# S5 parameters in large stores, later state loads, one weight spill and a carried-over stage in a hybrid streaming encoder step

## Chip, cores and metric

The kernel runs on 1 core of one Trainium2 chip. The metric is the device time of one execution in microseconds (us); less is better. The five engines are TensorE (PE), VectorE (DVE), ScalarE (ACT), GpSimd (POOL) and SyncE (SP). SP and POOL issue the transfers here.

## What is computed

One layer of a two-branch encoder on 2048 prompt frames and 8 x 16 sample frames of width 1024, in float32. Cut to what matters:

```python
h = rmsnorm(x, ln_g)
u_a, z_a, u_b, z_b, g_a, g_b = split(h @ w_in)     # 512, 512, 1024, 1024, 1024, 1024 columns
# branch A: S5 with 32 groups of 16 channels, 64 complex states each
y_a = gelu(s5_scan(u_a, state_s5))                 # B, C and lambda of each group, D u
y_a = y_a * sigmoid(y_a @ w_glu + b_glu)
p_a = (y_a * silu(z_a)) @ w_pa
# branch B: causal convolution of width 4, RG-LRU
xc = conv(u_b, state_conv)
y_b = rglru(xc, state_lru)                         # a = exp(-8 r softplus(-lam)), r and i by block-diagonal gates
p_b = (y_b * silu(z_b)) @ w_pb
m = sigmoid(g_a) * p_a + sigmoid(g_b) * p_b
y = rmsnorm(x + m @ w_out)
```

The last states of both recurrences and of the convolution are outputs too.

## The kernel before

**Tiles.** The 2176 frames are five tiles: four of 512 frames and one of 128, the sample (TILES, NT = 5). Each float32 operand is held as two float16 parts, high and low, and each product is three passes (L159 to L161: high x high, high x low, low x high), so a 128x512 product over 1024 rows is 24 matmuls. Five PSUM banks with the tag mm take the products, three with the tag a the small ones.

**Stages.** (1) The frames are normed and transposed, and u_a is computed (uE, four tiles of 8704 bytes per partition, m = 0 to 3). During the fourth tile SP stores each uE[m] to uD (L594) while POOL and DVE finish the S5 parameters in the job `params`, which ends with nine stores by SP to the DRAM tile parD (L513 to L523). parD holds 16 sets of 453 numbers per partition, so each store is cut into 128 x 16 pieces of 4 to 512 bytes. (2) The pools of stage 1 close, and the pools pgb (pages) and gp open on their memory; gp has 21 slots with the tag g, which `gt` takes, on the side where uE lay. The first lines after this load the states of the LRU and the convolution and clear and fill the small tile dn (L630 to L642). (3) Two loops over the five tiles compute gate B's first four column blocks (`direct`), with W0, then with W1; beside them run the jobs `t_forms`, which form the sums of a Strassen-Winograd product, and the splitting of W1. In the second loop, after tile 2, `lru_states` transposes the states on PE. (4) Branch B: 16 pairs of column blocks, 8 of branch B in turn with 8 of the gates (`run_pair`, seven products for each half of the tiles, positions 1 to 7 and 9 to 15, the sample at 8). (5) Projection B (y_b @ w_pb): the loop over n and m, 24 matmuls each. (6) The GLU and projection A (`ga_tile`: 4 products with w_glu, then 8 with w_pa), and the output (`out_tile`).

**What sets the order.** The program is issued in the order in which it is written; each engine and each queue takes its instructions in that order. Beside the products runs a planner. Jobs are generators in the lists tasks and low; `pump(budget)` takes one step of each job that is due, tasks first, until the budget is used up. A step that yields Later(k) rests k ticks, Step(c) costs c and rests one tick. A tick comes after each product: 2.4 less what the product's own eviction costs in branch B, 2.2 in projection B (`beside`, twice in each (n, m), once at n = 4). Tiles of a pool are freed by their last use, so a new tile in a slot waits for what used the slot before, a store's landing too.

**The jobs.** `b_work` is the elementwise part and the scan of one block of branch B; its last stage y_lo stores y to ybD (L976). `w_spill` loads 44 blocks of w_pb, w_glu, w_pa and w_out (L1151), splits each into high and low (scopy, stt) and stores it (L1159); it is put into low twice: before `load_pair(0)`, and again with `s5_prep` after tile 2 of the second loop. `s5_prep` (two of them, the second from the end of branch B on) reads a parameter set (L1195), rests 3 ticks, and makes the matrices wb and wc, the kernel kf and its shifted form dd of two groups. `s5_run(q)`, 16 jobs that are started 4 ticks apart in projection B, at most three at a time, reads them (sp, u and the phases ph, L1391 to L1395), rests 5 ticks, and runs the scan:

```python
while q not in prepared or running > 2:
    yield Later(1)
running += 1
...
yield Later(5)
...
    running -= g
```

**The end of branch B.** In the last pair, `hook_z` loads the pages of w_pb at positions 8 to 11. At 13 it runs the planner until tasks is empty, loads y_b of tile 0 (`y_load(0)`) and the S5 state (`s5_open`, h0n). After the pair come `s5_init` (two transposes of h0n on PE), `y_load(NT - 1)` and projection B. `out_states` (three transposes on PE, copies `so` on DVE) stands at n = 0, m = 3. Behind the loop `beside` runs until no job is left.

**The GLU operand.** `glu_prep(n)` loads ya, the scan's output of tile n in four parts (L1615), and splits it into yh (8 copies on ACT, 8 subtractions on DVE). For tile 0 it stands ahead of everything; for tile n + 1 it and ga_tile(n + 1) are one chain, of which two steps are taken after each product group of out_tile(n).

Of the kernel before, what the change touches and what calls it, by code (L numbers as in the profile page):

```python
# [43 lines left out]
O_PR, O_PI, O_B, O_BS, O_C, O_CS, O_ER, O_EI, O_M = 0, 34, 68, 100, 132, 164, 196, 324, 452  # L44
NPAR = 453
# [3 lines left out]
def build(tc, I, O):  # L49
# [30 lines left out]
    with ExitStack() as es:  # L80
# [3 lines left out]
        wp = es.enter_context(tc.tile_pool(name="wp", bufs=1))  # L84
# [22 lines left out]
        l16 = cp.tile([P, 2, 16], F32, name="l16")  # L107


        uD = dr.tile([512 * 8, 544], F16, name="uD")  # L110
        parD = dr.tile([16, P, NPAR], F32, name="parD")
# [101 lines left out]
        with ExitStack() as p1x:  # L213
# [25 lines left out]
            m16c = p1.tile([P, 16], F32, name="m16c")  # L239
# [58 lines left out]
            def params():  # L298
# [171 lines left out]
                pv = parD.rearrange("q p x -> p q x")  # L470

# [158 lines left out]
        rows2 = gt([64, P], F32, name="rows2")  # L630
        SP.dma_start(out=rows2, in_=I["state_lru"][0].rearrange("s (b c) -> (s b) c", c=P))
        rows3 = [gt([96, P], F32, name=f"rows3{i}") for i in range(2)]
        cst = I["state_conv"][0].rearrange("s k (b c) -> (s k b) c", c=P)
        for i in range(2):
            SP.dma_start(out=rows3[i], in_=cst[96 * i:96 * i + 96])

        dn = gt([16, 64], name="dn")
        V.memset(dn, 0.0)
        s5d = I["s5_d"][0].rearrange("(q g) h -> q g h", g=2)
        SP.dma_start(out=dn[:, 0:16], in_=s5d[:, 0])  # L640
        SP.dma_start(out=dn[:, 48:64], in_=s5d[:, 1])
        SP.dma_start(out=e16, in_=I["c_e16"])  # L642
# [260 lines left out]

        def b_work(b, ns):
# [69 lines left out]
            def y_lo(n):  # L974
                tt(y[n][:, 1], h.pop(n), y[n][:, 0], SUB)
                G.dma_start(out=ybD[n, b] if n < NT - 1 else ybS[b], in_=y.pop(n))  # L976

# [152 lines left out]
        def w_spill():  # L1130
# [15 lines left out]
            for i, (src, dst, nk) in enumerate(blocks):  # L1146
# [3 lines left out]
                raw = gt([P, nk, 512 // nk], name="wr")  # L1150
                SP.dma_start(out=raw, in_=src)  # L1151
                yield Later(2)
                while busy(NO_SPILL):
                    yield Later(1)
                q = gt([P, nk, 2, 512 // nk], F16, name="wq")
# [3 lines left out]
                G.dma_start(out=dst, in_=q)  # L1159
                yield Step(0.7)  # L1160
            done["spill"] = len(blocks)
# [13 lines left out]
        def s5_prep(second):  # L1175
# [12 lines left out]
            while todo:  # L1188
# [118 lines left out]
        low.append([0, w_spill()])  # L1307
# [3 lines left out]
        for n in range(NT):  # L1311
            for i in range(2):
# [210 lines left out]

        def wpb_load():
            wpb.append(page_load(page_b("t0", (2, KB, 2, P), "wpb"), wpbD[len(wpb)]))

        def y_load(n):
            for h in range(2):
                if n < NT - 1:
# [280 lines left out]
```

## Time and profile before

| | us |
|---|---|
| median of 3 runs | 1629.98 (1626.01 to 1632.69) |
| the profiled execution's own time | 1622.52 |
| its span, first to last instruction | 1620.7 |
| TensorE busy | 1457.7 (90%) |
| VectorE busy | 1063.9 (66%) |
| ScalarE busy | 839.9 (52%) |
| GpSimd busy | 301.7 (19%) |

The profile is of one execution. Its page gives busy times, the span in 40 slices, and the costliest groups; the list of waits tells for whom an engine stood idle; the timeline gives instructions in order of time, with the idle time before them in brackets; stage windows give busy times of a stretch. PEclk is the clock granted to TensorE, 1.00 being 2.4 GHz and 0.50 being 1.2 GHz. A wait for several semaphores is put down to the one that came last.

### The profile page before, as it was taken

What the parts mean: (1) busy time and instruction counts of PE and PEld (TensorE: products, weight loads), DVE (VectorE), ACT (ScalarE), POOL (GpSimd) and SP (SyncE); (2) the same over time, 40 slices, a digit from 0 to 9 for tenths busy, and PEclk for the clock granted to TensorE, in tenths of its full rate; (3) what the DMA queues carried; (4) which work ended last, traced back from release to release, by engine and by line L of the source; (5) the groups of instructions that cost most, each with busy time, mean ns of one, the idle gap of its engine ahead of it and who ended that gap; (6) DMA issues with size and microseconds to landing.
All of it is one profiled execution on the core that took longest, in us unless ns stands there. A gap on an engine that the chain in (4) does not pass through costs nothing.

```text
span 1620.7 us, 23021 instructions
## 1 busy us (share of the span) xinstructions
PE 1457.7 (90%) x8168; PEld 727.1 (45%) x8168; DVE 1063.9 (66%) x2181; ACT 839.9 (52%) x1570; POOL 301.7 (19%) x601
## 2 busy tenths in 40 slices
PE   6992699999989999999999895799999799999997
PEld 4440244444444444444444442355556444343444
DVE  6540585876867686786868685456765775656554
ACT  7540233675857676775858474143434452424232
POOL 0770011021111202020111102244444200000000
PEclk9996799999999999999999997899999799999999
DMA  7229522334342514243333408888978833333432
GB/s 198 88 86 99 126 75 95 103 111 129 109 142 86 165 53 163 88 146 92 114 123 115 141 22 306 319 289 303 308 266 308 314 130 137 122 138 122 138 105 79
DMA packets 194412, 245.31 MB, mean 151 GB/s; under 512 B 42522, under 2 KB 139434, under 8 KB 192376
## 3 DMA queue, kind: packets, MB, share of 16 engines
q1 hardware_dynamic: 166840, 162.51, 34.1%
q0 software_dynamic: 27456, 81.32, 13.7%
q8 instruction: 64, 1.05, 0.3%
q14 instruction: 52, 0.43, 0.1%
HBM read 145.40 MB, written 98.38 MB: 150 GB/s over the span
## 4 chain that ended last, share of the span: by engine, by line
PE 46%; DVE 16%; issue 10%; DMA 6%; ACT 5%; POOL 1%; SPq 1%; POOLq 0%; ACTq 0%; DVEq 0%
PE ps_mm L160 11%; PE ps_mm L161 11%; PE ps_mm L159 11%; PE ps_mm L1729 3%; PE ps_mm L1727 3%; PE ps_mm L1728 3%; DVE xc L66 2%; DVE wf L66 2%; DMA par<-parD 1%; DMA ya<-yDp 1%; DVE q L887 1%; DMA mbD<-gb 1%; DVE yh L54 1%; ACT yh L75 1%; DMA h0n<-state_s 1%
## 5 line engine op out<-in xcount | busy, mean ns | idle before, releaser
L161 PE MATMUL ps_mm<-h,wf 128*128 128x512 f16 x448 | 170.7, 381 | 42.3 <-DVE wf L66 42.3
L159 PE MATMUL ps_mm<-T,wf 128*128 128x512 f16 x512 | 194.5, 380 | 2.2 <-DVE gs L54 1.9
L161 PE MATMUL ps_mm<-T,wf 128*128 128x512 f16 x512 | 194.5, 380 | 1.0 <-DVE wf L66 1.0
L160 PE MATMUL ps_mm<-T,wf 128*128 128x512 f16 x512 | 194.5, 380 | 0.0
L161 PEld LDWEIGHTS <-wf 128*128 128x128 f16 x1232 | 121.3, 98 | 158.3 <-DVE wf L66 44.3
L159 PEld LDWEIGHTS <-wf 128*128 128x128 f16 x1232 | 121.4, 99 | 116.9 <-issue 5.4
L160 PEld LDWEIGHTS <-wf 128*128 128x128 f16 x1232 | 121.3, 98 | 114.8 <-issue 6.6
L159 PE MATMUL ps_mm<-h,wf 128*128 128x512 f16 x448 | 170.9, 381 | 2.0 <-ACT wf L75 2.0
L160 PE MATMUL ps_mm<-h,wf 128*128 128x512 f16 x448 | 170.8, 381 | 0.0
L75 ACT ACT_TABLE_LOAD x64 | 82.1, 1283 | 51.0 <-PE ps_mm L161 49.4
L1729 PE MATMUL ps_mm<-wo,M 128*128 128x512 f16 (+2 forms) x280 | 104.0, 373 | 0.1
L1727 PE MATMUL ps_mm<-wo,M 128*128 128x512 f16 (+2 forms) x280 | 104.1, 373 | 0.0
L1728 PE MATMUL ps_mm<-wo,M 128*128 128x512 f16 (+2 forms) x280 | 104.1, 373 | 0.0
L159 PE MATMUL ps_mm<-Y,wpb 128*128 128x512 f16 x256 | 100.1, 391 | 0.0
L160 PE MATMUL ps_mm<-Y,wpb 128*128 128x512 f16 x256 | 99.6, 389 | 0.0
L161 PE MATMUL ps_mm<-Y,wpb 128*128 128x512 f16 x256 | 99.4, 388 | 0.0
L75 ACT ACTIVATE wq<-wr 128x512 f16<-128x512 f32 x88 | 53.2, 619 | 42.4 <-DMA wr<-w_out 25.8
L66 DVE SCALAR_TENSOR_TENSOR xc<-ub,PC,xc 128x512 f32<-128x512 f32 x96 | 71.9, 749 | 2.3
L66 DVE SCALAR_TENSOR_TENSOR xo<-ps_mm,xo 128x512 f32<-128x512 f32 (+2 forms) x35 | 24.9, 711 | 65.9 <-PE ps_mm L1729 65.9
L66 DVE SCALAR_TENSOR_TENSOR wq<-wr,wq 128x512 f16<-128x512 f32 x88 | 59.1, 685 | 11.4 <-ACT wq L75 11.0
L160 PE MATMUL ps_mm<-yA,wt 128*128 128x512 f16 (+1 forms) x160 | 54.9, 351 | 9.8 <-DVE yA L66 9.8
L66 DVE SCALAR_TENSOR_TENSOR wf<-wraw,wf 128x512 f16<-128x512 f32 (+1 forms) x82 | 55.7, 696 | 10.8 <-ACT wf L75 10.8
(316 smaller groups left out, 3294.9 us busy)
## 6 DMA issues: line engine op xcount, KB each, us to landing
wraw<-w_in SPq DMA_DIRECT2D x38, 512.0 KB, 3.9
sp<-sD SPq DMA_DIRECT2D x16, 768.0 KB, 6.4
xt<-x_prompt SPq DMA_DIRECT2D x16, 512.0 KB, 4.2
gbD<-gs POOLq DMA_DIRECT2D x32, 256.0 KB, 2.4
wr<-w_pb SPq DMA_DIRECT2D x32, 256.0 KB, 3.4
wpbD<-wq POOLq DMA_DIRECT2D x32, 256.0 KB, 3.1
ybD<-y POOLq DMA_DIRECT2D x32, 256.0 KB, 3.3
gaD<-gs POOLq DMA_DIRECT2D x32, 256.0 KB, 2.7
```

The costliest lines, as they stand in the source:

```text
L54: V.tensor_tensor(out=out, in0=a, in1=b, op=op)
L66: V.scalar_tensor_tensor(out=out, in0=a, scalar=s, in1=b, op0=op0, op1=op1)
L75: S.activation(out=out, in_=a, func=f, **kw)
L159: PE.matmul(p, lhsT=a[:, 0], rhs=b[:, 0], start=first, stop=False, skip_group_check=more)
L160: PE.matmul(p, lhsT=a[:, 0], rhs=b[:, 1], start=False, stop=False, skip_group_check=more)
L161: PE.matmul(p, lhsT=a[:, 1], rhs=b[:, 0], start=False, stop=last, skip_group_check=more)
L887: V.tensor_tensor_scan(out=q, data0=a, data1=q, initial=0.0 if n == 0 else prev[:, w - 1:w], op0=MUL, op1=ADD)
L1727: PE.matmul(p, lhsT=lh[0], rhs=w_[:, 0, c], start=(k == 0), stop=False)
L1728: PE.matmul(p, lhsT=lh[0], rhs=w_[:, 1, c], start=False, stop=False)
L1729: PE.matmul(p, lhsT=lh[1], rhs=w_[:, 0, c], start=False, stop=(k == KB - 1))
```

## The change

parD becomes three DRAM tiles with the partition first, written by five stores and read in parts; m16c stays in SBUF (pool cp). The state loads move into `load_states`, which is called at n = 1 of the second loop. One `w_spill` is left; outside branch B it uses tiles of pool wp and loads one block ahead. At the end of branch B the jobs are not run out any more: `y_load` waits (in the program's order) only for the blocks that it reads, `s5_open` moves to position 9, `y_load(NT - 1)` into projection B, `out_states` to n = 1. A parameter set rests 6 ticks outside branch B, a scan's pages 7. `glu_prep` runs a tile further ahead, its subtractions one turn later.

```diff
-        wp = es.enter_context(tc.tile_pool(name="wp", bufs=1))
+        wp = es.enter_context(tc.tile_pool(name="wp", bufs=1, reuse_waits="tile"))
...
-        parD = dr.tile([16, P, NPAR], F32, name="parD")
+        pwD = dr.tile([P, 2, 16, 34], F32, name="pwD")
+        bcD = dr.tile([P, 4, 16, 32], F32, name="bcD")
+        etD = dr.tile([P, 2, 16, P], F32, name="etD")
...
-                SP.dma_start(out=pv[:, :, O_PR:O_PR + 34], in_=pw[:, 0].rearrange("p (q g) e -> p q (g e)", g=2))
-                SP.dma_start(out=pv[:, :, O_PI:O_PI + 34], in_=pw[:, 1].rearrange("p (q g) e -> p q (g e)", g=2))
-                for o, src in ((O_B, bst), (O_BS, bsw)):
-                    SP.dma_start(out=pv[:, :, o:o + 32], in_=src.rearrange("p (q g) h -> p q (g h)", g=2))
-                for o, src in ((O_C, cc[:, 0]), (O_CS, cc[:, 1])):
-                    SP.dma_start(out=pv[:, :, o:o + 32], in_=src.rearrange("p (q x) -> p q x", x=32))
+                SP.dma_start(out=pwD, in_=pw.rearrange("p r (q g) e -> p r q (g e)", g=2))
+                for o, src in enumerate((bst, bsw)):
+                    SP.dma_start(out=bcD[:, o], in_=src.rearrange("p (q g) h -> p q (g h)", g=2))
+                SP.dma_start(out=bcD[:, 2:4], in_=cc.rearrange("p i (q x) -> p i q x", x=32))
                 level(64, 63, tt)
                 yield
-                SP.dma_start(out=pv[:, :, O_ER:O_ER + P], in_=et[:, 0])
-                SP.dma_start(out=pv[:, :, O_EI:O_EI + P], in_=et[:, 1])
-                SP.dma_start(out=pv[:, :, O_M], in_=m16c)
+                SP.dma_start(out=etD, in_=et)
...
+        def load_states():
+            nonlocal rows2, rows3, dn
...
+            dn = gt([16, 64], name="dn")
+            V.memset(dn, 0.0)
...
+                if branch_b:
+                    r = gt([P, nk, 512 // nk], name="wr")
+                else:
+                    r = raw_tile()[:, 0:4].rearrange("p a b -> p (a b)").rearrange("p (k c) -> p k c", k=nk)
...
+                raw = nxt
+                if raw is None:
+                    raw = load(i)
+                    yield Later(2 if branch_b else 6)
+                nxt = None if branch_b or i + 1 == len(blocks) else load(i + 1)
...
+                    q = wp.tile([P, nk, 2, 512 // nk], F16, tag="wt", name="wq", bufs=1)
...
-                par = gt([P, O_ER], name="par")
-                SP.dma_start(out=par, in_=parD[q, :, 0:O_ER])
-                yield Later(3)
+                par = gt([P, NPAR], name="par")
+                SP.dma_start(out=par[:, 0:68].rearrange("p (r e) -> p r e", r=2), in_=pwD[:, :, q])
+                SP.dma_start(out=par[:, 68:196].rearrange("p (i x) -> p i x", i=4), in_=bcD[:, :, q])
+                yield Later(3 if branch_b else 6)
...
-        low.append([0, w_spill()])
         raw = load_pair(0)
...
+            if n == 1:
+                load_states()
...
-            SP.dma_start(out=ph, in_=parD[q, :, O_ER:NPAR])
-            yield Later(5)
+            SP.dma_start(out=ph.rearrange("p (r c) -> p r c", r=2), in_=etD[:, :, q])
+            yield Later(7)
...
         def y_load(n):
+            while (7, n) not in stored:
+                beside()
...
+            if pos == 9:
+                s5_open()
             if pos == 13:
-                while tasks:
-                    clock += 1
-                    pump(1e9)
                 y_load(0)
-                s5_open()
...
-        y_load(NT - 1)
...
-        PAGES = {(0, 2): [lambda: y_load(1)], (0, 6): [lambda: y_load(2)], (1, 2): [lambda: y_load(3)],
+        PAGES = {(0, 1): [lambda: y_load(NT - 1)], (0, 2): [lambda: y_load(1)], (0, 6): [lambda: y_load(2)], (1, 2): [lambda: y_load(3)],
...
-                if n == 0 and m == 3:
+                if n == 1 and m == 3:
                     out_states()
...
-                for j in range(2):
-                    tt(tv[1][:, j], yv[:, j], tv[0][:, j], SUB)
+
+                def low(tv=tv, yv=yv):
+                    for j in range(2):
+                        tt(tv[1][:, j], yv[:, j], tv[0][:, j], SUB)
+                defer(1, low)
...
+        flush()
+        ahead = glu_prep(1)
         for i, _ in enumerate(ga_tile(0)):
...
+            if i > 7:
+                next(ahead, None)
         for n in range(NT):
             flush()
-            nxt = chain(glu_prep(n + 1), ga_tile(n + 1)) if n + 1 < NT else iter(())
-            for _ in out_tile(n):
+            nxt = ga_tile(n + 1) if n + 1 < NT else iter(())
+            for i, _ in enumerate(out_tile(n)):
                 for _ in range(2):
                     pump(0)
                     next(nxt, None)
+                if i == 3 and n + 2 < NT:
+                    ahead = glu_prep(n + 2)
+                if i > 3:
+                    next(ahead, None)
```

## Rows read from the trace of the kernel before

**Rows 1.** The page: busy time, share of the span and instructions of each engine.
```profile
PE 1457.7 (90%) x8168; PEld 727.1 (45%) x8168; DVE 1063.9 (66%) x2181; ACT 839.9 (52%) x1570; POOL 301.7 (19%) x601
```

**Rows 2.** Stage window: length, busy PE, PEld, DVE, ACT, POOL, granted clock, DMA share, GB/s.
```profile
160.00:200.00 40.00, 24.90 (x107) 10.98 (x108) 20.61 (x33) 9.23 (x14) 2.25 (x4) 0.76 0.58 135
```

**Rows 3.** List of waits, 118 to 205 us: us in total, times, longest.
```profile
PE ps_mm L161 <- DVE wf L66: 42.3, 1, 42.3
```

**Rows 4.** Timeline, 118 to 200 us: start, us, engine, line, operation, [idle before <- releaser].
```profile
121.11 3.81 SPq L516 DMA_DIRECT2D parD<-bst  x1
...
162.00 5.88 SPq L594 DMA_DIRECT2D uD<-uE  x2
...
173.38 0.11 DVE L638 MEMSET dn<- 16x64 f32 x1 [41.74 <-DMA uD<-uE]
...
175.10 0.61 PE L161 MATMUL ps_mm<-h,wf 128*128 128x512 f16 x1 [42.34 <-DVE wf L66]
...
178.92 0.41 PE L161 MATMUL ps_mm<-h,wf 128*128 128x512 f16 x1
```

**Rows 5.** List of waits, PE alone, 200 to 960 us: the largest kind.
```profile
PE ps_a L160 <- DVE xs L54: 19.7, 9, 3.9
```

**Rows 6.** List of waits, PE alone, 960 to 1290 us: the four largest kinds.
```profile
PE ps_a L170 <- DVE wb L54: 11.7, 3, 9.0
PE ps_a L1251 <- DVE wc L54: 9.2, 3, 5.5
PE ps_a L170 <- DVE so L1480: 7.9, 1, 7.9
PE ps_a L170 <- DMA h0n<-state_s: 5.6, 1, 5.6
```

**Rows 7.** Timeline, 990 to 1022 us: PE at the carry into projection B.
```profile
998.59 0.38 PE L161 MATMUL ps_mm<-T,wf 128*128 128x512 f16 x1
...
1015.14 0.63 PE L159 MATMUL ps_mm<-Y,wpb 128*128 128x512 f16 x1
...
1018.55 0.42 PE L161 MATMUL ps_mm<-Y,wpb 128*128 128x512 f16 x1
```

**Rows 8.** Timeline, 1245 to 1300 us: the last scan run on PE, POOL and SP.
```profile
1251.96 0.87 PE L1403 MATMUL ps_a<-u,sp 128*128 128x136 f16 x12
...
1267.24 0.76 POOL L1463 DMA_DIRECT2D yDp<-yo  x1
...
1259.56 12.36 SPq L1615 DMA_DIRECT2D ya<-yDp  x4
```

**Rows 9.** Timeline of PE: first and last high pass of two GLU products, tiles 1 and 2.
```profile
1328.82 0.38 PE L159 MATMUL ps_mm<-yh,wt 128*128 128x512 f16 x1
...
1333.35 0.38 PE L159 MATMUL ps_mm<-yh,wt 128*128 128x512 f16 x1
...
1403.82 0.38 PE L159 MATMUL ps_mm<-yh,wt 128*128 128x512 f16 x1
...
1414.90 0.38 PE L159 MATMUL ps_mm<-yh,wt 128*128 128x512 f16 x1
```

**Rows 10.** Groups by line: count, busy us, mean ns of one, idle before and releaser.
```profile
L66 DVE SCALAR_TENSOR_TENSOR wq<-wr,wq 128x512 f16<-128x512 f32 x88 | 59.1, 685 | 11.4 <-ACT wq L75 11.0
...
L75 ACT ACTIVATE wq<-wr 128x512 f16<-128x512 f32 x88 | 53.2, 619 | 42.4 <-DMA wr<-w_out 25.8 <-DMA wr<-w_pa 11.9 <-DMA wr<-w_pb 1.9
...
L54 DVE TENSOR_TENSOR yh<-ya,yh 128x256 f16<-128x256 f32 (+1 forms) x40 | 39.4, 1162 | 15.4 <-ACT yh L75 15.4
```

**Rows 11.** Views of the tiles par, parD and Y: time from issue to landing.
```profile
DMA to landing us min/median/max: 2.7/3.5/6.3
...
DMA to landing us min/median/max: 2.7/6.3/19.7
...
DMA to landing us min/median/max: 8.7/12.3/15.0
```

**Rows 12.** Stage window 1262 to 1266 us, columns as in rows 2.
```profile
1262.00:1266.00 4.00, 3.73 (x62) 3.55 (x60) 0.52 (x3) 0.92 (x4) 2.10 (x4) 1.00 0.98 314
```

More of the change, by code (lines that the diff above doesn't have):

```diff
@@ L41 @@
 KS = 2.0 ** 10
[L44 to L45 removed]
+O_PR, O_PI, O_B, O_BS, O_C, O_CS, NPAR = 0, 34, 68, 100, 132, 164, 196
 PREP_WAIT = 6
@@ L107, in build @@
         l16 = cp.tile([P, 2, 16], F32, name="l16")
+        m16c = cp.tile([P, 16], F32, name="m16c")
         uD = dr.tile([512 * 8, 544], F16, name="uD")
-        parD = dr.tile([16, P, NPAR], F32, name="parD")
+        pwD = dr.tile([P, 2, 16, 34], F32, name="pwD")
+        bcD = dr.tile([P, 4, 16, 32], F32, name="bcD")
+        etD = dr.tile([P, 2, 16, P], F32, name="etD")
         kpD = dr.tile([16, 2, 16, 2, 384], F16, name="kpD")
@@ L629, in build @@
         CT = lrs[:, 328:544].rearrange("p (s k b) -> p s k b", s=1 + NS, k=3)
[L630 to L642, printed above, removed]
+        rows2 = rows3 = dn = None
+        def load_states():
+            nonlocal rows2, rows3, dn
+            rows2 = gt([64, P], F32, name="rows2")
+            SP.dma_start(out=rows2, in_=I["state_lru"][0].rearrange("s (b c) -> (s b) c", c=P))
+            rows3 = [gt([96, P], F32, name=f"rows3{i}") for i in range(2)]
+            cst = I["state_conv"][0].rearrange("s k (b c) -> (s k b) c", c=P)
+            for i in range(2):
+                SP.dma_start(out=rows3[i], in_=cst[96 * i:96 * i + 96])
+            dn = gt([16, 64], name="dn")
+            V.memset(dn, 0.0)
+            s5d = I["s5_d"][0].rearrange("(q g) h -> q g h", g=2)
+            SP.dma_start(out=dn[:, 0:16], in_=s5d[:, 0])
+            SP.dma_start(out=dn[:, 48:64], in_=s5d[:, 1])
+            SP.dma_start(out=e16, in_=I["c_e16"])
         def lru_states():
@@ L902, in scan_tile @@
             return gx
+        stored = set()
         def b_work(b, ns):
@@ L976, in y_lo @@
                 G.dma_start(out=ybD[n, b] if n < NT - 1 else ybS[b], in_=y.pop(n))
+                stored.add((b, n))
             stages = [(taps, 2.0), (xs_hi, 0.1), (xs_lo, 0.7), (gates, 0.4), (input_gate, 0.7), (decay, 0.2),
@@ L1145, in w_spill, with load @@
                                    woD[k // 2, :, k % 2, None, :, c], 1))
-            for i, (src, dst, nk) in enumerate(blocks):
+            def load(i):
+                src, _, nk = blocks[i]
+                if branch_b:
+                    r = gt([P, nk, 512 // nk], name="wr")
+                else:
+                    r = raw_tile()[:, 0:4].rearrange("p a b -> p (a b)").rearrange("p (k c) -> p k c", k=nk)
+                SP.dma_start(out=r, in_=src)
+                return r
+            nxt = None
+            for i, (_, dst, nk) in enumerate(blocks):
                 done["spill"] = i
@@ L1159, in w_spill @@
                 G.dma_start(out=dst, in_=q)
+                del raw, q
                 yield Step(0.7)
+                if nxt is not None:
+                    yield Later(2)
             done["spill"] = len(blocks)
@@ L1525, in wpb_load, with beside @@
             wpb.append(page_load(page_b("t0", (2, KB, 2, P), "wpb"), wpbD[len(wpb)]))
+        def beside():
+            nonlocal clock
+            clock += 1
+            pump(2.2)
         def y_load(n):
+            while (7, n) not in stored:
+                beside()
             for h in range(2):
@@ L1579, in build @@
         gb_load()
-        def beside():
-            nonlocal clock
-            clock += 1
-            pump(2.2)
         for n in range(NT):
```

15 lines of the change are left out of this document (6 added, 9 removed).

## Prediction

> **What bounds the kernel now.** Read the page first: TensorE (PE) is busy for 1457.7 of 1620.7 us and no other engine for more than 66% [rows 1], so what is to be had is the 163 us in which PE stands, and the time after each stand in which it is granted 1.2 instead of 2.4 GHz (a granted clock of 0.76 in the mean from 160 to 200 us, [rows 2]). The list of waits says where: one wait of PE for VectorE (DVE) is 42.3 us long [rows 3]. The timeline there [rows 4] shows where it comes from. A clearing of the small tile dn stands in DVE's order ahead of the weight split; dn lies on memory of uE, so it waits 41.7 us for the last two stores of uE (issued at 162.00, gone at 173.4); the split that PE needs stands behind it, and PE goes on at 175.10. Those stores are late because SP issues one transfer after the other and has nine parameter stores among them; one that is shown kept it 3.8 us.
>
> After this, the same list for PE alone: in branch B only short waits, the largest kind 19.7 us in nine [rows 5]; from 960 us on four kinds that add up to 34.4 us [rows 6]. The timeline of the carry into projection B [rows 7], the end of projection B [rows 8] and the GLU products [rows 9] give the rest. A matmul of 512 columns at full pace takes 0.2157 us: 21 of them lie between the first two rows of [rows 9], (1333.35 - 1328.82) / 21. A tick of the planner beside 12 of them is thus 2.6 us.
>
> **The parts, worked out (gains are positive).**
>
> *Parameter stores and small states.* Nine stores of 2048 pieces each (128 partitions x 16), 18,432 pieces of 4 to 512 B, become five stores whose pieces are 2 to 16 KB. SP is then free when the last uE is written, and dn is cleared a loop later. Of the wait, 42.3 us go, and the slow start: nine matmuls from 175.10 to 178.92 took 3.8 us instead of 9 x 0.2157, 1.9 us more. What is late next: the first tiles of pool gp still lie on uE. PE's wait begins at 132.8 (175.10 - 42.34), and the last uE is written by then; if its store takes the 11.4 us from 162.00 to 173.4, DVE and ScalarE (ACT) may write gp at 144. PE needs its split, some 2 us after 132.8, and then has five PSUM banks of 24 matmuls, 5 x 5.2 = 26 us, before it must wait for them: until 160. I charge 3 us for the split and for DVE starting 8 us behind; bounds 1 and 10. The new place of the state loads is behind the W1 splits on SP and four products ahead of their use; dn's clearing on DVE has matmuls of the second loop beside it: nothing, or some 2 us of PE waiting for the transposes. **+41**.
>
> *Spill once.* The trace has 88 of each of the two operations on wq [rows 10], twice the 44 blocks. Gone are 44 x 619 ns on ACT (27 us), 44 x 685 ns on DVE (30 us), 44 loads on SP and 44 stores on POOL. All lie beside matmuls, so the worth is that of PE's short waits. By counting ticks (one step of a job per tick, 2.4 less the eviction's cost in each) some 34 blocks and 12 parameter sets are through at the end of branch B, where 62 blocks and 10 sets are now: DVE's freed time goes half into earlier sets. The 5.5 us wait at wc (DVE waited there for a tile that a store held, [rows 6]) has fewer tiles to wait for. I take 3 of the 19.7 us and 4 of this wait with its slow clock; bounds -5 and +15. **+7**. Waits counted by tile for pool wp, m16c in pool cp: nothing, since wp opens before any pool is closed and m16c is 64 B; no row bounds the first, I keep 2 us either way for it.
>
> *Parameter reads in small pieces.* Each of 16 sets is now read by two loads, 256 pieces of 136 B and 512 of 128 B, instead of 128 of 784 B; the phase table by 256 pieces instead of 128; 16 more issues. Price: 2048 pieces of 128 B kept SP 3.81 us [rows 4], so 768 are 1.4 us of SP, 23 us over all 16, beside some 800 us in which SP mostly waits. Landing was 3.5 us in the median and 6.3 at most [rows 11]; with 768/2048 of the 19.7 us that a parameter store took at worst, it would be 7.4 + 3.5 = 10.9 us. Between the two I take 5 us: it stays under the three ticks, 7.8 us, that the job leaves. Nothing; upper bound 16 x 3.1 = 50 us. The Trainium skill speaks against this edit: "DMA: Bandwidth & Descriptors", Specifications, sets 512 B as the least piece for full rate, because a smaller one is read, changed and written. By it the 12,288 new pieces are as dear as the stores taken away were, and the sum would be 25 instead of 75. That rival stands below.
>
> *Branch B's end carried over.* PE's last product of pair 15 begins at 998.59 and the first of projection B at 1015.14: 16.2 us after its end. Then 8 matmuls take 3.4 us instead of 1.7 [rows 7]. In the gap are waits of 9.0 us for wb and 5.6 us for h0n [rows 6], the rest is transposes; both loads stood behind the drain in SP's order. Now h0n goes out at position 9 instead of 13, some 13 us earlier, and no set is rushed. What is late next is Y: two loads at position 13, 5.2 us ahead of PE's end, landing in 8.7 to 15.0 us [rows 11]. At 8.7 PE waits 3.5 us, at 15 about 10; the jobs' dd loads ahead on SP can hold them up further. I take 5 us of waiting with its clock: 14.6 + 1.7 - 5, **+11**; bounds 2 and 16.
>
> *Longer lead in projection B, output of states one tile later.* The wait of 7.9 us at so [rows 6] is DVE standing for a parameter set; it goes with six ticks of lead (15.6 us) for three. The rest of wb and wc there, 11.7 - 9.0 and 9.2 - 5.5, together 6.4 us, loses competitors: spills that now use wraw and wt instead of gp's tiles. I take 7.9, 2 of clock and half of 6.4: **+13**; bounds 4 and 16.
>
> *The scan's tail.* A scan run holds one of three places from its loads for 5 + 6 ticks; now for 7 + 6. Starts were 4 ticks apart (11 < 12), the last at tick 60, its first matmul at 65 of the loop's 72. Now three start every 13 ticks and a little, the last at 66, its first matmul at 73: behind projection B. Before, that matmul was at 1251.96 and the last store at 1267.24, and the last of four ya loads left when it had landed, at 1271.9 (1259.56 + 12.36) [rows 8]. PE was done at 1265.7 [rows 12], some 2 us of it for this run, so projection B alone ends near 1264. Of the 15.3 us from matmul to store I leave 11, since no other work takes turns with it any more: the store goes out at 1275 instead of 1267.24. **-8**; bounds -15 (the chain as it is) and -4.
>
> *GLU operand one stage ahead.* Tile 1's two GLU products run at full pace; tile 2's need 1414.90 - 1403.82 = 11.1 us for the 21 matmuls that take 4.5 [rows 9]. Tile 3 repeats this, tile 4 does not. That is 2 x 6.6 = 13 us. Tile 1's splits now fall beside tile 0's last products; eight DVE operations of 1.16 us [rows 10], 9.3 us, come on top there: I charge 2 us of waiting before the first output. **+11**; bounds 6 and 13.
>
> Sum: 41 + 7 + 11 + 13 - 8 + 11 = 75. Against the profiled execution's 1622.5 us that is 1547.5; the median of the runs shown is 7.5 us above it, so **1555 us**.
>
> **Rivals.**
>
> 1. *The first wait only changes its tile* (gp's first writer instead of dn). It decides if uE's last store lands after 160, 28 us after its write against 11.4 now; at worst all 41 us stay: 1596. Against it: only two large stores stand ahead on SP. 7%.
> 2. *Small pieces make the reads late.* 3.1 us of PE at each of up to 16 sets: 1605, at half of it 1580. For it: 12,288 pieces under 512 B. Against it: the job runs three ticks, later six, ahead. The rule of the Trainium skill named above is this mechanism; no read in such pieces stands in this trace. 7%; with rival 1 together 3% (about 1621, no change).
> 3. *The carry gives nothing*, since SP sends Y only behind dd loads and PE waits as now: 1566. 13%.
> 4. *The freed time shows*: most of branch B's short waits go, 15 us more: 1540. 8%.
> 5. *Slower*: the scan's pages land after their seven ticks (18 us), and each of 16 runs stops PE, which takes its matmuls in order. It decides at 75 / 16 = 4.7 us each, so at a landing of 23 us: 1630 and more. The longest landing in [rows 11] is 19.7 and the loads of Y, the largest, need 15.0. 2%.
>
> That the second spill goes is plain from the count of 88, so the edit does what it says.
>
> **The numbers.** Forecast 60%, rivals as given. Its own bounds are about 1533 to 1578; to leave out no more than 2 in 10 the range reaches to rival 2's half and the carry's failure: 1533 to 1592. Half a per cent is 8 us, about what a measurement of this kernel can tell from no change: faster by more 95%, within it 3%, slower 2%.
>
> **What would show it.** Right: no wait over 10 us for dn or the first gp writer before 180 us; 44 operations on wq; PE's gap at the carry under 8 us; the last scan matmul behind projection B, with a gap of some 20 us before the GLU; tile 2's 21 matmuls in 4.5 us. Wrong: a 30 us wait for uE under another name; DVE waiting for par in branch B; Y issued behind dd.

## Result and profile after

The changed kernel takes 1582.97 us in the median of 3 runs (1578.47 to 1584.21), against 1629.98 before: a ratio of 0.9707, 95% interval [0.9664, 0.9751], a gain of 47 us where 75 were forecast. It lies in the range (1533 to 1592), 28 us above the forecast. The profiled execution has a span of 1581.2 us, 39.5 less than that of before.

The page of the changed kernel, its busy times, answers to [rows 1]; the stage window 160 to 200 us to [rows 2]:

```profile
PE 1456.8 (92%) x8168; PEld 727.6 (46%) x8168; DVE 1038.7 (66%) x2137; ACT 813.8 (51%) x1524; POOL 275.1 (17%) x557
```

```profile
160.00:200.00 40.00, 40.00 (x223) 19.61 (x221) 32.58 (x54) 15.62 (x28) 4.29 (x8) 1.00 0.23 73
```

TensorE does the same 8168 matmuls in the same busy time (0.9 us less), so nearly all of the gain is idle time: 163.0 us before, 124.4 now. Where it is, the stages tell. Each is cut at the start of a matmul that both kernels have: the first with W0; the first with T; the last of pair 15; the first and the last 512-wide one of projection B; the first with yh; and at the end of the last of all. The rows of the runs described below are already in the table (us):

| profile of | start to W0 | W0 to T | branch B | gap | projection B | tail | GLU and output | median of runs |
|---|---|---|---|---|---|---|---|---|
| before | 132.2 | 139.6 | 726.8 | 16.5 | 235.3 | 19.6 | 344.1 | 1629.98 |
| changed | 138.3 | 95.8 | 748.3 | 0.4 | 218.2 | 33.5 | 339.9 | 1582.97 |
| e1_lock | 137.7 | 95.8 | 717.7 | 12.5 | 221.2 | 33.2 | 341.6 | 1565.11 |
| e2_spill2 | 137.9 | 95.8 | 765.7 | 1.8 | 218.9 | 34.6 | 339.9 | 1603.52 |
| e3_later5 | 137.8 | 95.9 | 748.5 | 0.5 | 219.7 | 20.9 | 340.3 | 1576.21 |
| e4_glulate | 138.8 | 95.7 | 747.9 | 0.4 | 215.2 | 33.6 | 333.5 | 1575.51 |
| e5_before_once | 139.1 | 142.4 | 752.0 | 15.3 | 216.6 | 18.9 | 344.6 | 1638.76 |
| e6_lock_y11 | 138.9 | 95.7 | 717.6 | 0.5 | 226.6 | 33.7 | 341.1 | 1562.13 |
| e7_all | 134.8 | 97.9 | 717.2 | 0.5 | 233.7 | 19.2 | 337.7 | 1550.84 |
| e8_first | 133.3 | 95.7 | 732.6 | 16.7 | 237.5 | 20.5 | 345.3 | 1589.76 |
| e9_two | 136.9 | 95.7 | 731.5 | 1.1 | 223.8 | 18.6 | 334.6 | 1550.96 |
| e10_two | 134.1 | 98.3 | 742.0 | 1.8 | 228.9 | 21.3 | 333.4 | 1573.47 |
| e11_lead3 | 141.1 | 98.3 | 749.2 | 0.5 | 223.8 | 33.6 | 339.4 | 1591.15 |
| e12_two14 | 137.7 | 95.7 | 723.8 | 0.4 | 228.2 | 19.4 | 337.0 | 1551.64 |

Between before and changed: 43.8 gained at the first wait, 21.5 *lost* in branch B, 16.1 gained at the gap, 17.1 in projection B, 13.9 lost in the tail, 4.2 gained in the output, together 45.8. The stretch up to W0, 6.1 longer, is treated at the end. How far single profiles agree can be seen where kernels have the same program: branch B is 747.9 to 749.2 in changed, e3_later5, e4_glulate and e11_lead3, but projection B is 218.2 in changed and 215.2 in e4_glulate. A difference of 3 us in projection B can be nothing.

**The first wait.** The list of waits, 118 to 205 us, has in the place of the 42.3 us of [rows 3] only 0.7 us; these lines of it bear on the change:

```profile
DVE hw L53 <- DMA uD<-uE: 5.4, 1, 5.4
...
PE ps_mm L161 <- ACT wf L74: 2.0, 1, 2.0
...
PE ps_mm L163 <- DVE wf L65: 0.7, 1, 0.7
```

The timeline of SP there answers to [rows 4]: the store of bst, which kept SP 3.81 us, takes 0.85, and the last two uE leave at 132.71 instead of 162.00.

```profile
123.22 0.85 SPq L514 DMA_DIRECT2D bcD<-bst  x1
...
132.71 5.46 SPq L589 DMA_DIRECT2D uD<-uE  x2
```

**Branch B.** The list of waits, TensorE alone, over the whole of branch B: 271 to 999 us in the kernel before, then 234 to 983 us in the changed one:

```profile
PE ps_a L160 <- DVE xs L54: 19.7, 9, 3.9
PE ps_a L1251 <- DVE wc L54: 6.9, 2, 5.5
PE ps_a L170 <- DVE wb L54: 5.9, 6, 4.0
```

```profile
PE ps_a L1272 <- DVE wc L53: 15.7, 8, 3.7
PE ps_a L162 <- DVE xs L53: 15.0, 9, 2.5
PE ps_a L172 <- DVE wb L53: 11.1, 6, 3.3
```

The waits for wb and wc, the outer products of the parameter sets, go from 12.8 to 26.8 us, 14.0 more. (The recorded texts below name 11.1 us in 6 and 13.7 in 7: the window 200 to 920 us, without the end of branch B.) The timeline of one such wait in the changed kernel shows what VectorE did:

```profile
583.71 0.44 DVE L898 TENSOR_TENSOR_SCAN gx<-ax,gx 128x136 f32<-128x136 f32 x1 [4.01 <-ACT ax L74]
584.18 0.18 DVE L69 TENSOR_SCALAR lrs<-gx 128x8 f32<-128x8 f32 x1
584.27 0.68 DVE L65 SCALAR_TENSOR_TENSOR q<-q,xc 128x512 f32<-128x512 f32 x1
584.87 0.75 DVE L53 TENSOR_TENSOR wc<-par 128x256 f32<-128x256 f32 x2
...
586.32 0.69 DVE L53 TENSOR_TENSOR wc<-wc,t 128x512 f32<-128x512 f32 x1
...
587.07 0.42 PE L1272 MATMUL ps_a<-wc,par 128*32 128x128 f32 x1 [3.68 <-DVE wc L53]
```

VectorE was not busy: it stood 4.0 us for the copy ax of the sample's scan on ScalarE, with wc behind it in its order, and TensorE's products of wc stand one tick behind wc in its own. The stand for ax is in the kernel before too (the view of tile ax: 29.4 us in 8 there, 28.1 us in 8 here). There wc began 4.4 us behind the scan gx, with eight other operations between:

```profile
701.96 0.44 DVE L899 TENSOR_TENSOR_SCAN gx<-ax,gx 128x136 f32<-128x136 f32 x1 [4.01 <-ACT ax L75]
...
706.33 0.75 DVE L54 TENSOR_TENSOR wc<-par 128x256 f32<-128x256 f32 x2
```

In the changed kernel wb or wc begins 1.2 us behind gx at four of the eight stands (gx at 488, 584, 769 and 863 us), and TensorE waits 3.3 to 3.7 us there each time, 14.0 us in all. The other 12.8 us are ten waits elsewhere, the longest 3.3 us.

```profile
  ACT ax L75: 29.4, 8
```

```profile
  ACT ax L74: 28.1, 8
```

**The spill.** The groups by line answer to [rows 10]: 34 and 10 conversions of wq on VectorE instead of 88.

```profile
L65 DVE SCALAR_TENSOR_TENSOR wq<-wr,wq 128x512 f16<-128x512 f32 x34 | 23.2, 683 | 2.3 <-ACT wq L74 2.3
...
L65 DVE SCALAR_TENSOR_TENSOR wq<-wraw,wq 128x512 f16<-128x512 f32 x10 | 6.9, 689 | 2.1 <-DMA sp<-etD 1.3 <-ACT wq L74 0.6
```

**Parameter reads.** The view of tile par answers to the first line of [rows 11]: the two loads of a set, in pieces of 136 and 128 B, land in 2.6 us in the median, where the one load in pieces of 784 B took 3.5.

```profile
DMA to landing us min/median/max: 2.2/2.6/4.8
```

VectorE waits for par twice in branch B, 4.0 and 2.5 us, which the prediction named as a sign of being wrong; but TensorE's waits for wb behind them are 0.4 us at most, and e5_before_once, with the loads of the kernel before, has two of 2.6 and 2.0 us.

**The tail.** The timeline of the changed kernel at the end of projection B, answering to [rows 8]; its last 512-wide product begins at 1201.1, and the products of the sample (with hs) follow:

```profile
1198.04 0.87 PE L1425 MATMUL ps_a<-u,sp 128*128 128x136 f16 x12
...
1216.24 0.22 PE L163 MATMUL ps_mm<-hs,wpb 128*128 128x128 f16 x1
...
1218.05 0.87 PE L1425 MATMUL ps_a<-u,sp 128*128 128x136 f16 x12
...
1228.74 0.77 POOL L1485 DMA_DIRECT2D yDp<-yo  x1 [0.41 <-ACT yo L74]
...
1234.67 0.58 PE L161 MATMUL ps_mm<-yh,wt 128*128 128x512 f16 x1 [6.64 <-ACT yh L74]
```

From the last run's first matmul to its store it is 10.7 us (15.3 before). That matmul comes 1.6 us after the sample's last product, with which projection B ends, so the store comes 12.3 us after it. In the kernel before that product was the line below, the store came 1.5 us after it (at 1267.24, [rows 8]), and the first GLU product 2.8 us after the store instead of 5.9 now.

```profile
1265.51 0.22 PE L161 MATMUL ps_mm<-hs,wpb 128*128 128x128 f16 x1
```

**The output.** The timeline of VectorE and TensorE behind tile 0's last GLU products:

```profile
1283.04 2.31 DVE L53 TENSOR_TENSOR yh<-ya,yh 128x256 f16<-128x256 f32 x2
1284.96 0.90 DVE L65 SCALAR_TENSOR_TENSOR M<-ga,M 128x512 f16<-128x512 f32 x1
1285.78 2.31 DVE L53 TENSOR_TENSOR yh<-ya,yh 128x256 f16<-128x256 f32 x2
1287.71 0.90 DVE L65 SCALAR_TENSOR_TENSOR M<-ga,M 128x512 f16<-128x512 f32 x1
...
1288.66 0.61 PE L1753 MATMUL ps_mm<-wo,M 128*128 128x512 f16 x1 [1.28 <-DVE M L65]
```

Between the operands M that TensorE needs now stand tile 1's splits, which it needs much later. The 0.61 us of that matmul is the lower clock (0.38 us otherwise); three such waits, 5.3 us, stand at the first output. The GLU of tile 2, which took 11.1 us for 21 matmuls in [rows 9], takes 5.5 and has one short wait left:

```profile
1365.58 0.38 PE L161 MATMUL ps_mm<-yh,wt 128*128 128x512 f16 x1
...
1368.68 0.38 PE L162 MATMUL ps_mm<-yh,wt 128*128 128x512 f16 x1 [0.78 <-DVE yh L53]
...
1371.06 0.38 PE L161 MATMUL ps_mm<-yh,wt 128*128 128x512 f16 x1
```

### The profile page after: what moved, and what is told of

Its sections match the earlier page's. It is cut to its first block, busy times and chain, and to the rows that moved or that the text cites. A ratio compares the mean times of both kernels' runs of the same rounds, so it can differ in the third digit from the quotient of the medians.

```text
span 1581.2 us, 22662 instructions
## 1 busy us (share of the span) xinstructions
PE 1456.8 (92%) x8168; PEld 727.6 (46%) x8168; DVE 1038.7 (66%) x2137; ACT 813.8 (51%) x1524; POOL 275.1 (17%) x557
## 4 chain that ended last, share of the span: by engine, by line
PE 55%; DVE 19%; issue 12%; ACT 7%; DMA 4%; POOL 2%; SPq 1%; DVEq 0%; POOLq 0%; ACTq 0%
PE ps_mm L162 14%; PE ps_mm L161 14%; PE ps_mm L163 14%; PE ps_mm L1753 3%; PE ps_mm L1751 3%; PE ps_mm L1752 3%; DVE xc L65 3%; DVE wf L65 2%; DVE yh L53 2%; ACT L74 1%; PE ps_a L1272 1%; ACT pt L74 1%; DVE sz L65 1%; DVE wc L53 1%; DVE q L65 1%
## 5 line engine op out<-in xcount | busy, mean ns | idle before, releaser
L162 PEld LDWEIGHTS <-wf 128*128 128x128 f16 x1232 | 121.5, 99 | 118.6 <-issue 11.7
L161 PE MATMUL ps_mm<-h,wf 128*128 128x512 f16 x448 | 173.2, 387 | 2.0 <-ACT wf L74 2.0
L163 PE MATMUL ps_mm<-h,wf 128*128 128x512 f16 x448 | 172.5, 385 | 0.7 <-DVE wf L65 0.7
L162 PE MATMUL ps_mm<-h,wf 128*128 128x512 f16 x448 | 172.9, 386 | 0.0
L161 PE MATMUL ps_mm<-Y,wpb 128*128 128x512 f16 x256 | 97.8, 382 | 0.4 <-DMA Y<-ybD 0.4
L162 PE MATMUL ps_mm<-Y,wpb 128*128 128x512 f16 x256 | 97.8, 382 | 0.0
L163 PE MATMUL ps_mm<-Y,wpb 128*128 128x512 f16 x256 | 97.6, 381 | 0.0
L65 DVE SCALAR_TENSOR_TENSOR gb<-gb,ps_mm 128x512 f32<-128x512 f32 (+1 forms) x40 | 24.1, 606 | 92.2 <-PE ps_mm L163 74.7
L74 ACT ACTIVATE gs<-ps_mm 128x512 f32<-128x512 f32 (+1 forms) x92 | 48.1, 532 | 44.8 <-PE ps_mm L163 39.3
```

Source lines behind the costliest of these rows:

```text
L65: V.scalar_tensor_tensor(out=out, in0=a, scalar=s, in1=b, op0=op0, op1=op1)
L74: S.activation(out=out, in_=a, func=f, **kw)
L161: PE.matmul(p, lhsT=a[:, 0], rhs=b[:, 0], start=first, stop=False, skip_group_check=more)
L162: PE.matmul(p, lhsT=a[:, 0], rhs=b[:, 1], start=False, stop=False, skip_group_check=more)
L163: PE.matmul(p, lhsT=a[:, 1], rhs=b[:, 0], start=False, stop=last, skip_group_check=more)
```

## Experiments

None of these kernels leaves out part of the computation. Each ratio is to the kernel before, run beside that kernel (medians of 1628.5 to 1632.6 us). A position is the place of a tick among the 30 of two pairs: 1 to 15 in a pair of branch B, 16 to 30 in the gate pair after it.

**e1_lock.** Are the parameter sets at the wrong place?

```diff
-        NO_PREP = range(11, 19)
+        NO_PREP = range(11, 24)
```

> One number of the changed kernel: the steps that make wb and wc may not start at positions 11 to 23 of the 30 of two pairs (11 to 18 in the changed kernel). Theory P (place): in branch B the outer products for wb and wc (six VectorE operations each) now start in ticks whose budget is nearly used up, and TensorE's transposes or products of them stand one tick behind in its order; with the second spill gone nothing holds them back from position 22. Locked as before to one set per two pairs, the waits of TensorE for wb (11.1 us in 6, 200 to 920 us) and wc (13.7 us in 7) fall to under 3 us each, branch B (first product with T to the last product of pair 15) goes from 748.7 us to 727 to 733, and the time falls by 14 to 21 us, to about 1562 to 1569. Nine sets instead of twelve are then through at its end, which may give 0 to 5 us back in projection B. Rival R (reads and tiles): the parameter reads in small pieces or the tile pools hold the jobs up; then the positions change little, branch B stays within 4 us of 748.7 and the time within 5 us of 1583.

Measured 1565.11 us (1563.49 to 1568.54), ratio to before 0.9594 [0.9569, 0.9619]. Branch B is 717.7 us, 30.6 less than in the changed kernel and 9.1 less than in the kernel before. Its list of waits, 233 to 952 us:

```profile
PE ps_a L162 <- DVE xs L53: 19.4, 9, 3.6
PE ps_a L172 <- DVE wb L53: 4.1, 8, 1.3
PE ps_a L1272 <- DVE wc L53: 2.5, 3, 1.5
```

VectorE's stand for ax is as long as ever, 28.9 us in 8, and TensorE has no wait of over 1.5 us for wb or wc left: 6.6 us together, 26.8 in the changed kernel. Theory P holds for the waits and the time; branch B fell further than it gave. But the lock moves more than the place: 9 sets are made in branch B instead of 12. The stage windows of branch B (changed kernel, e1_lock, e9_two; columns as in [rows 2]) show what that is worth:

```profile
234.20:982.50 748.30, 701.16 (x3877) 342.44 (x3876) 554.74 (x1029) 498.68 (x870) 110.22 (x204) 0.98 0.32 104
233.50:951.20 717.70, 689.45 (x3828) 336.84 (x3827) 536.88 (x990) 485.78 (x854) 103.26 (x191) 0.99 0.31 101
232.60:964.10 731.50, 699.85 (x3876) 342.59 (x3875) 553.99 (x1032) 494.86 (x870) 110.29 (x204) 0.98 0.33 104
```

Of the 30.6 us, 18.9 are idle time of TensorE; in the other 11.7 it works, on the three sets' 48 matmuls and at a granted clock of 0.98 instead of 0.99. e9_two, described below, makes 12 sets in branch B with the positions locked, and so parts the two: it is 16.8 us shorter than the changed kernel, 15.5 of it idle time. That is the place. It is 14.3 us longer than e7_all, from which it differs only in when the second parameter job begins. That is the three sets.

A new wait of 11.9 us came with the lock, at the carry. The list of waits of SP, 935 to 960 us, and the timeline of SP and TensorE:

```profile
SPq L1290 <- DMA kpD<-kh: 13.2, 1, 13.2
```

```profile
951.51 2.61 SPq L1290 DMA_DIRECT2D dd<-kpD  x4
954.17 1.63 SPq L1543 DMA_DIRECT2D Y<-ybD  x2
...
963.70 0.58 PE L161 MATMUL ps_mm<-Y,wpb 128*128 128x512 f16 x1 [11.89 <-DMA Y<-ybD]
```

Y stands in SP's order behind dd loads that wait for a store: the prediction's third rival, which the changed kernel only just misses (there Y left at 971.38, 11.5 us ahead of its product).

**e2_spill2** puts the work of a second spill back into branch B, without holding the sets.

```diff
+                    low.append([0, w_spill(True)])
                     low.append([0, w_spill()])
```

(with True, the job runs only in branch B, and its counter isn't used)

> The changed kernel with a second spill job beside the first one, in branch B only (some 26 blocks more are loaded, split and stored once again, with the same contents), so that ScalarE, VectorE and the queues have about the work of the kernel before. By a count of ticks the parameter sets start at the same positions as in the changed kernel (wb at 22, wc at 22 and 5). Theory P (place): the work is not what matters; branch B stays at 746 to 756 us and the waits for wb and wc stay above 20 us together; the time is within 8 us of 1583 (the extra job may lengthen it a little). Rival W (work): what changed is the load beside the matmuls, for example that work taken away lets the clock or the jobs run differently; then branch B returns to 727 to 735 us and the time falls by 13 us or more.

Measured 1603.52 us, ratio 0.9847 [0.9806, 0.9888]. Branch B did not shrink but grew to 765.7; the waits for wb and wc are 36.9 us there (22.5 and 14.4). Rival W falls. So does P's "the work is not what matters": the 25 conversions that come back into branch B (58 instead of 33) lengthen it by 17.4 us. And a second job ahead of the sets does not by itself bring their old places back: at four of the eight stands TensorE still waits 3.3 to 3.7 us right behind ax.

**e3_later5** undoes one number of the scan.

```diff
-            yield Later(7)
+            yield Later(5)
```

> One number of the changed kernel: a scan run rests 5 ticks after its loads instead of 7, as in the kernel before. Theory T (tail): the last of the 16 runs then starts its matmuls inside projection B instead of behind it (a count of ticks gives 0 instead of 8 ticks after the loop), the gap from the last product of projection B to the first GLU product goes from 33.4 us to 18 to 23, and the time falls by 10 to 15 us, to about 1568 to 1573. Rival L (landing): the pages of a run (sp, u, ph) land late by 5 ticks and each of 16 runs stops TensorE; then waits for sp or u appear in projection B, it grows by 8 us or more from 218 us, and the time is within 5 us of 1583.

Measured 1576.21 us, ratio 0.9663 [0.9631, 0.9696]: the tail fell from 33.5 to 20.9 us, projection B rose by 1.5. Theory T holds for the tail, but the time falls by less than its 10 to 15 us: the median is 6.8 us under the changed kernel's, the profiled span 10.6. Rival L's sign appears once, a wait of 5.3 us for u in projection B, where the changed kernel had one of 4.8 us for ACT's v.

**e4_glulate** moves tile 1's eight subtractions behind tile 0's M, and begins tile 1's GLU one output group later.

```diff
-                defer(1, low)
+                defer(1 if n != 1 else 7 - m, low)
...
-                    next(nxt, None)
+                    if n or i:
+                        next(nxt, None)
```

> The changed kernel with the eight VectorE subtractions of the GLU operand of tile 1 put behind all eight operands M of tile 0 instead of between them, and the GLU of tile 1 begun one output group (of 24 matmuls) later. Theory M: the new waits of TensorE for M ahead of the first outputs (5.3 us in 3) and the low clock behind them (0.89 from 1277 to 1307 us) come from these subtractions; they go, and the time falls by 6 to 10 us, to about 1573 to 1577. Rival N: the wait only moves to the GLU operand of tile 1 (9.3 us of subtractions, one output group of 5.2 us ahead of it): waits for yh of 4 us or more appear there and the time falls by under 3 us.

Measured 1575.51 us, ratio 0.9655 [0.9622, 0.9687]. Waits for M are 0.5 us (5.3 in the changed kernel), waits for yh behind tile 0 are 3.7 (1.5), and the stage is 6.4 us shorter. Theory M, with a little of N.

**e5_before_once** takes one spill job from the kernel before, and nothing else.

```diff
-        low.append([0, w_spill()])
         raw = load_pair(0)
```

> The kernel before with its first spill job left out, nothing else. Theory P (place): with one spill job ahead of them in the list the parameter sets lose their fixed place; a count of ticks puts wb at 22, then wc at 22 and 5, as in the changed kernel. Branch B (first product with T to the last product of pair 15) grows from 726.8 us to 740 to 755 although 88 conversions less are made, the waits for wb and wc in it go from some 12 to 20 us or more, and the time goes up by 8 to 22 us against 1631. Rival R (what makes branch B longer in the changed kernel is another of its edits: the reads in small pieces, the tiles of pool wp, the earlier states): branch B falls by 5 to 10 us, and the time is 0 to 10 us under 1631. Besides, the first product with W0 began at 132.2 us in the kernel before and at 137.7 to 138.8 in all kernels of the changed family, on the same order of instructions; if that hangs on the family it begins at 132 to 133 here, if it varies by run it need not.

Measured 1638.76 us in 10 runs, ratio 1.005 [1.0033, 1.0068]: less work, and slower. Branch B grew by 25.2 us to 752.0; its list of waits, 281 to 1034 us, is close to that of the changed kernel:

```profile
PE ps_a L1251 <- DVE wc L54: 18.7, 8, 4.6
PE ps_a L160 <- DVE xs L54: 14.9, 9, 2.5
PE ps_a L170 <- DVE wb L54: 10.9, 5, 3.5
```

It makes 12 sets in branch B, as the changed kernel does, and at four stands TensorE waits 3.3 to 3.7 us right behind ax. That settles which edit cost branch B its time: the spill job, by the sets' place and number together. The total rose by only 6 to 9 us because projection B fell by 18.7, with the old lead and the old place of the states' output.

**e8_first** makes the first part alone: large stores, small-piece reads, later states. Its edit is the diff's lines for pwD, bcD, etD, m16c and `load_states`.

> The kernel before with the first part of the change alone: large parameter stores, the reads from them in small pieces, and the states loaded at the second product loop; both spill jobs, the drain at the end of branch B, the rest of 3 and 5 ticks and the old GLU chain stay. Theory P: the first wait goes (W0 to the first product with T from 139.6 to 95 to 99 us) and nothing else moves: branch B stays at 724 to 732 us, although all parameter reads are now in pieces of 128 and 136 B; the time is 39 to 45 us under that of the kernel before, 1586 to 1592, so that the other parts of the change together are worth only 3 to 9 us. Rival R (small pieces): DVE waits for par at each of 16 sets, branch B grows by 10 to 25 us, and the time is only 15 to 33 us under that of the kernel before.

Measured 1589.76 us, ratio 0.9745 [0.9695, 0.9795]. The first wait went (95.7 us), and branch B is 732.6, 5.8 more than before and just over what P allowed. Its sets and conversions are as many as before, and its waits for wb and wc hardly more (13.9 us against 12.8), so the 5.8 us stay unexplained. This first part is worth 43 us; all other parts together 7, which the two intervals do not tell from nothing.

**e11_lead3** puts the lead of the sets and the place of `out_states` back in the changed kernel.

```diff
-                yield Later(3 if branch_b else 6)
+                yield Later(3)
...
-                if n == 1 and m == 3:
+                if n == 0 and m == 3:
```

> The changed kernel with the lead of the parameter sets in projection B and the place of the states' output put back: rest of 3 ticks everywhere, out_states at the fourth block of the first tile. Theory S (jobs left): projection B's first 512-wide products to its last took 235.3 us before, 218.2 in the changed kernel, and 216.6 where only one spill job was taken from the kernel before, so it is short because fewer spills and sets are left to be done in it. Here it stays at 215 to 223 us and the time within 5 us of 1583. Rival L (lead, as the prediction had it): the waits for so (7.9 us before) and par come back and projection B grows by 8 to 15 us, the time to 1590 to 1598.

Measured 1591.15 us, ratio 0.9742 [0.9715, 0.9769]. Projection B is 223.8 us, 5.6 more than in the changed kernel: just outside what S gave, short of L's 8 to 15. But the time is L's, and so is the mechanism: VectorE stands for par there for 5.8, 1.3 and 6.3 us, which it does not in the changed kernel, and TensorE waits 7.1 us for wb and 5.7 for wc behind it. None of the waits is for so. With 3 us between like stages the 5.6 is rough, and the intervals of the two times overlap.

**e6_lock_y11, e7_all, e9_two, e10_two, e12_two14** look for a better version.

```diff
+            if pos == 11:
+                y_load(0)
             if 7 < pos < 12:
                 wpb_load()
...
-            if pos == 13:
-                y_load(0)
```

> The kernel with the places held (positions 11 to 23), and the two loads of Y of tile 0 moved from position 13 of the last pair to 11, ahead of the last page of w_pb. Theory Q (queue): the 11.9 us that TensorE waited for Y there came from SP's order: Y stood behind four dd loads that waited for the stores of kh (SP stood from 938 to 951 us) and left at 954 instead of some 939. Now Y lands before projection B, the gap ahead of it falls from 12.5 us to under 4, and the time by 8 to 12 us, to about 1553 to 1557. Rival D: the loads of Y are slow by themselves (15 us and more beside the other traffic), the wait stays above 7 us and the time within 4 us of 1565.

Measured 1562.13 us, ratio 0.9585 [0.9553, 0.9616]. The gap fell from 12.5 to 0.5 us, so Q is right about the queue, and wrong about the time: projection B grew by 5.4, with waits for wb of 5.5 and 4.5 us. A reading that no run tests: while TensorE stood for Y the jobs had caught up; now they are late.

> The candidate: the places held (11 to 23), Y of tile 0 at position 11, a scan run's rest of 5 ticks, and the subtractions of the GLU operand of tile 1 behind M of tile 0. If the four causes are apart, their gains add: 1565 less 10 (Y), less 6 to 10 (the tail; a count of ticks leaves 4 ticks of it, since only 9 sets are through at the end of branch B), less 7 (GLU) = 1538 to 1544. If they hang together (the tail comes back because sets are late), 1548 to 1556.

Measured 1550.84 us (1548.32 to 1556.28), ratio 0.9521 [0.9486, 0.9556]; the second forecast holds. The tail fell to 19.2 us, but projection B rose to 233.7: with 9 sets done instead of 12, and the scans closer together, TensorE waits 13.1 us there, all for wb and wc. By the ratios it is some 30 us better than the changed kernel all the same.

e9_two lets the second parameter job begin at the ninth pair (`while second and branch_b and pairs < 8`), e10_two closes positions 4 to 6 as well, e12_two14 is e9_two with the last pair but one (`pairs < 14`).

> The candidate of the run before, with the second parameter job begun at the ninth pair of branch B instead of at its end. In the candidate only 9 sets were through there, and projection B took 233.7 us against 218.2 in the changed kernel, with waits for wb of 5.8 and 4.1 us. Theory S (sets left): projection B is short when few sets are left; a count of ticks gives 14 sets at its beginning, the second job's wb at position 5 and wc at 7. Projection B falls to 215 to 222 us, branch B grows by 1 to 5 us from 717.2, and the time falls from 1550.8 to 1537 to 1545. Rival W: the second set of each two pairs meets VectorE behind its work at position 5 (a wait of 1.4 us with its clock in the changed kernel) and the more of branch B is as large as the gain: 1548 to 1554.

> As the run before, with positions 4 to 6 closed to the parameter jobs too: the second job's wb falls on 7 or 2, its wc on 2 or 7, and 12 sets are through at the end of branch B by a count of ticks. Theory P (place): branch B is 1 to 4 us shorter than with positions 4 to 6 open, projection B 1 to 4 us longer, the time within 3 us of that run.

> The candidate with the second parameter job begun at the last but one pair of branch B (at the ninth it cost branch B 14.3 us and gave projection B 9.9). A count of ticks gives 11 sets at the end of branch B and no tick of tail. If the cost of a second set goes with the number of pairs that hold one, branch B grows by 2 to 4 us from 717.2 and projection B falls by 4 to 9 from 233.7: 1544 to 1550. If the gain and the cost are equal for each set, 1549 to 1553.

Measured 1550.96 us (0.9519 [0.9488, 0.9549]), 1573.47 (0.9669 [0.9646, 0.9692]) and 1551.64 (0.9505 [0.9488, 0.9523]). e9_two made 12 sets in branch B, not the 14 of the count, and moved 14.3 us into it and 9.9 out of projection B; its time is that of Rival W. e12_two14 made 10, not 11, and moved 6.6 and 5.5. A set costs branch B somewhat more than it saves projection B, and the time stays within 1 us of the candidate's. e10_two contradicts its expectation by 22 us: branch B grew to 742.0, with waits for ScalarE's gs (2.4, 1.1, 1.7, 1.8 us) where the changed kernel has none and e9_two one of 0.5. Why two jobs together do that was not followed up. Not tried: the sample's copy ax on another engine or earlier, so that VectorE would not stand for it.

## Why the prediction was right in sign and 28 us too hopeful

By its own steps, forecast and measured by stages:

- *Parameter stores and small states*: 41, measured 43.8, and in e8_first alone 43.9. What was to be late next is there, a 5.4 us wait of VectorE for uD, and TensorE does not feel it. **Right.**
- *Spill once*: 7, measured -21.5 in branch B. **This is the step that failed.** It said that the freed time goes "half into earlier sets" and gave those sets no price. Their count was nearly right (12 are made in branch B; before it was 9, where the count gave 10). What the runs show: with as many sets as before and their places held, branch B gains 9.1 (e1_lock against before, the other edits with it; forecast 7). The three earlier sets cost it 14.3 (e9_two against e7_all), of which projection B gives 9.9 back. And the places into which the sets fall cost 16.8 (changed kernel against e9_two), nearly all idle time of TensorE, 14.0 of it right behind VectorE's stands for ax. Together -22.0, against -21.5. The profile of before could have raised the question: 29.4 us in 8 stands of VectorE for ax lie there at a fixed place of every two pairs, with wc 4.4 us behind most of them. How the two spill jobs kept the sets at their places before is not shown: taking the first away loses the place (e5_before_once), but a second job put back does not restore it (e2_spill2).
- *Small pieces*: nothing, and nothing came: 2.6 us to landing. By the Trainium skill's rule ("DMA: Bandwidth & Descriptors", Specifications, 512 B as the least piece for full rate) the prediction had put the sum at 25. The trace does not bear that out for these reads: their time to landing did not rise with the number of pieces (2.6 us against 3.5). The measured time lies near the 1580 of rival 2's half, but its mechanism is absent: it falls by this row and by e8_first.
- *Carry*: 11, measured 16.1. The 5 us charged for Y did not come (a wait of 0.4 us); they come as 11.9 when the sets shift, as e1_lock shows, so rival 3 was missed by an accident of place.
- *Longer lead*: 13, measured 17.1, but mostly from another step. The mechanism is there: e11_lead3 takes the lead back, VectorE stands for par again and 5.6 us are lost. But e5_before_once has the old lead and a projection B shorter by 18.7 us, with 4 sets left for it instead of 7 and 10 conversions instead of 25. The two do not add, and what is no longer left over for projection B weighs more. The forecast asked for the worth of the spill in branch B and hardly here.
- *The tail*: -8, measured -13.9. The 11 us left of the chain were right (10.7), and so was the place of the last run, behind projection B. Three things the sum lacked: projection B without that run was to end near 1264, some 2 us sooner, but its last product lies 15.3 us behind the last wide one in both kernels; the run's first matmul comes 1.6 us after that, where the sum let it start at once; and the first GLU product comes 3.2 us later behind the last store than before, which was not taken apart. The bound of -15 held.
- *GLU one ahead*: 11, measured 4.2. The charge of 2 us for tile 1's splits on VectorE was too small: e4_glulate, which moves them, measures 6.4, and with it the stage's gain is 10.6.

Sum of the misses: +2.8, -28.5, +5.1, +4.1, -5.9, -6.8 = -29.2, which is 75 against 45.8. The steps are not apart: taken alone, the one spill made the whole kernel 0.5% slower (e5_before_once), some 8 us, where +7 was forecast.

## What to carry to other kernels

Work that is taken out of a planner's list lets the jobs behind it run sooner and elsewhere: give what runs sooner its price in the stage into which it moves, ask where each job now falls, and what its engine is *waiting* for there, not only how busy it is. An engine's harmless stand is harmless only as long as nothing that TensorE needs is issued right behind it; list such stands before moving anything. And cost a freed step in every later stage that would have inherited its rest, not only in the one where it ran.

## Not expected of the hardware

The first matmul with W0 began anywhere from 132.2 to 141.1 us in the 14 profiles, though up to there all have the same order of instructions on every engine but SP, which has the other parameter stores. The two kernels with the old stores have 132.2 and 139.1, the twelve with the new ones 133.3 to 141.1. It varies by execution (or by chip: the runs were made on several), so 6 us between two single profiles of this stretch can be nothing. The profiled execution of before had the earliest start of all, which may be most of the 7.5 us by which it lay under the median; the other executions of it left no trace to tell.
